# Splitting the weights into two float32r parts by transfers instead of by VectorE

## Chip, core and metric

The kernel runs on one core of a Trainium2 chip. The metric is the device time of one execution in microseconds; the median of two runs before the change is 1509.46 us (1509.07 and 1509.86). The profile is of one execution of its own, taken by the hardware profiler.

## What is computed

Two transformer blocks in a row on one sequence of 512 tokens and 1024 features, all in float32. The first has two mixers side by side (gated linear attention, and sparse attention with a compressed, a selected and a window branch), gates that merge them, and a SiLU feed-forward part 2816 wide. The second has two causal convolutions and stick-breaking attention as its mixer, and a squared-ReLU feed-forward part 4096 wide. Cut to the products with weights:

```python
proj = rms_norm(x, g) @ w_in                       # 1024 x 6440
x = x + rms_norm(mixed @ w_out, g_post)            # 1024 x 1024
f = (silu(h @ w_ffn_gate) * (h @ w_ffn_up)) @ w_ffn_down
p = _rmsnorm(x, g_attn) @ w_in_2
x = x + concat([y_a, y_b, y_c]) @ w_out_2
x = x + square(relu(h2 @ w_ff1_2)) @ w_ff2_2
```

## The kernel before

Every product is made as three float32r products: each operand is split into a high part (the value rounded to float32r) and a low part (what is left), and high by high, high by low and low by high are added up in PSUM. All weights are read from HBM once, in 228 pieces of 512 KB (a tile of 128 partitions x 1024 values), and three smaller pieces at the very start.

`load` (L122) makes one such piece. Its transfer (L125) is issued by SyncE into a staging tile `wst`, of which there are four. `split_w` (L110) then makes the high part `whi` by a casting copy on ScalarE (L113), and the low part `wlo` as `wst - whi` on VectorE (L114). There are four `whi` and four `wlo` as well, and they are given out in turn: the fifth piece takes the place of the first, once the products that read the first are done. Four weights of the second block go into tiles of their own, `early`, so that they can be split ahead of time.

Pieces have three shapes, by the stage that uses them. In the transposed projections (`proj_T`, L143, and `k_steps`, L157) a piece is 8 K tiles of 128 columns, 1024 rows of 512 bytes in HBM, and serves 24 matmuls of 512 columns. In the products in natural layout (`nat_half`, L215, and `half_steps`, L202) a piece is 2 K tiles of 512 columns, 256 rows of 2 KB; three or four pieces make a set, the set serves all four token tiles in turn, and so all pieces of a set are used until near the set's end. Eight pieces of the first block's output gate and four of `w_proj_nsa` are 4 K tiles of 256 columns, 512 rows of 1 KB. By shape there are 134, 82 and 12 pieces.

The kernel is written in program order, and a scheduler puts the instructions of each engine into that engine's queue; each queue is served in order. Beside the split, ScalarE and VectorE empty PSUM, make the activations and split those in the same way (`split_psum`, L135). GpSimd has the small steps of the norms (L240, L245, L246), masks and some set-up. The largest stages by weights are the first block's projections from the start on, its output projections and its feed-forward part (from about 395 to 905 us of the span), and the second block's feed-forward part (1105 to 1480 us); the attention stages lie between them.

Of the kernel before, what the change touches and what calls it, by code (L numbers as in the profile page):

```python
# [7 lines left out]
F32 = mybir.dt.float32  # L8
# [4 lines left out]
OP = mybir.AluOpType  # L13
# [7 lines left out]
def kernel(  # L21
# [78 lines left out]
    # the tensor engine's clock rises under load: products of zeros while the inputs are on their way  # L100
# [21 lines left out]
    def load(w, k0, kt, c0, n, step=1, pair=None):  # L122
        st = stage([128, kt, n])
        if step == 1:
            nc.sync.dma_start(st, w[k0 * 128:(k0 + kt) * 128, c0:c0 + n].rearrange("(k p) c -> p k c", p=128))  # L125
        else:
            for i in range(kt):
                k = k0 + i * step
                nc.sync.dma_start(st[:, i], w[k * 128:(k + 1) * 128, c0:c0 + n])
        return split_w(st, [128, kt, n], pair)  # L130
# [12 lines left out]
    def proj_T(acc, w, hT, cols=slice(0, 128), ts=slice(0, 512)):  # L143
        """acc[c, tok] = w[:, cols]^T h^T, the weights stationary."""
        wh, wl = w
        xh, xl = hT
        nk = wh.shape[1]
        for k in range(nk):
            mm(acc[:, ts], wh[:, k, cols], xh[:, k, ts], start=k == 0, stop=False)  # L149
            mm(acc[:, ts], wh[:, k, cols], xl[:, k, ts], start=False, stop=False)  # L150
            mm(acc[:, ts], wl[:, k, cols], xh[:, k, ts], start=False, stop=k == nk - 1)  # L151
# [5 lines left out]
    def k_steps(acc, w, hT):  # L157
        """the same, in steps of one K tile"""
        for k in range(8):
            mm(acc, w[0][:, k], hT[0][:, k], start=k == 0, stop=False)  # L160
            mm(acc, w[0][:, k], hT[1][:, k], start=False, stop=False)  # L161
            mm(acc, w[1][:, k], hT[0][:, k], start=False, stop=k == 7)  # L162
            yield

    def first_tiles(tiles, ahead=()):
        """The first products after a norm: all of the first 256 tokens, while the others are still on their way."""
        accs, ws = [], list(ahead)
        for i, (w, c0, tag) in enumerate(tiles):
            accs.append(ps(tag))
            if i >= len(ahead):  # L170
                ws.append(load_cols(w, c0))
            proj_T(accs[i], ws[i], hT, ts=slice(0, 256))
            if i in (0, 2):
                flush()
        for acc, w in zip(accs, ws):
            proj_T(acc, w, hT, ts=slice(256, 512))
        return accs

    def nat_mm(aT, acc, t, chunks, mid=lambda: None, cols=slice(None)):
        """acc[tok tile t, c] = sum_k a^T[k]^T w[k]; chunks: (list of k, split weights)"""  # L180
        s = slice(t * 128, (t + 1) * 128)
        seq = [(k, j, w) for ks, w in chunks for j, k in enumerate(ks)]
        for i, (k, j, (wh, wl)) in enumerate(seq):
            ah, al = aT(k)
            mm(acc, ah[:, s], wh[:, j, cols], start=i == 0, stop=False)  # L185
            mm(acc, ah[:, s], wl[:, j, cols], start=False, stop=False)  # L186
            mm(acc, al[:, s], wh[:, j, cols], start=False, stop=i == len(seq) - 1)  # L187
            if i == 1:
                mid()

    def nat_steps(aT, acc, t, chunks):
        """nat_mm in steps of one K tile"""
        s = slice(t * 128, (t + 1) * 128)
        seq = [(k, j, w) for ks, w in chunks for j, k in enumerate(ks)]
        for i, (k, j, (wh, wl)) in enumerate(seq):
            ah, al = aT(k)
            mm(acc, ah[:, s], wh[:, j, :], start=i == 0, stop=False)
            mm(acc, ah[:, s], wl[:, j, :], start=False, stop=False)
            mm(acc, al[:, s], wh[:, j, :], start=False, stop=i == len(seq) - 1)
            yield  # L200
# [9 lines left out]
    def natural(aT, w, ks, fin, c0=0, parts=None):  # L210
        """fin(t, half, acc) for both halves of 1024 columns, token tile by token tile."""
        for half in range(2):
            nat_half(aT, w, ks, fin, half, c0, parts)

    def nat_half(aT, w, ks, fin, half, c0=0, parts=None):  # L215
        chunks = []
        for i in range(0, len(ks), 2):
            kk = ks[i:i + 2]
            chunks.append((kk, load(w, kk[0], len(kk), c0 + half * 512, 512, step=max(kk[-1] - kk[0], 1))))
        for t in range(4):  # L220
            if t == 3 and half and parts:
                # in two, so that less is left to do after the last product
                for q in (slice(0, 256), slice(256, 512)):
                    acc = ps("mm", "nat")
                    nat_mm(aT, acc[:, q], t, chunks, cols=q)
                    parts(t, q, acc[:, q])
                return
            acc = ps("mm", "nat")
            nat_mm(aT, acc, t, chunks, lambda: flush(2))
            fin(t, half, acc)  # L230
# [4 lines left out]
    def half_sq(src, half, st):  # L235
        """mean of squares of one half row; eps goes in with the first half"""
        sq = small("sq")
        A.activation(ps("o", "junk"), src, AF.Square, scale=1.0 / 32, accum_out=sq)  # L238
        if half == 0:
            P.tensor_scalar(sq, sq, RMS_EPS, None, op0=OP.add)  # L240
        st[half] = sq
# [17 lines left out]
    def norm_T(t, g, hT):  # L259
        """RMS norm of token tile t of the residual, transposed into hT."""  # L260
# [18 lines left out]
    # transposes that wait for their norm: products that need not wait go first  # L279
# [9 lines left out]
    # =====================  block 1: mixers  =====================  # L289
# [86 lines left out]
    # transposed, with a row of ones for the bias  # L376
# [23 lines left out]
    def r_proj(hd):  # L400
        """x (1 + tanh(x / 2)) = 2 silu(x) of this head's output gate, natural layout"""
# [244 lines left out]
    def nsa_scores(h, bi):  # L646
        """softmax weights of one branch, gated; a step per query tile"""
# [27 lines left out]
    def nsa_values(h, bi):  # L675
        """the branch's weighted values, on top of the other branches'; a step per key tile and its products"""
# [46 lines left out]
    def merge_gates():  # L723
        """the gates of both mixers, in steps of one K tile"""
# [15 lines left out]
    # mn's tiles 2 p, 2 p + 1 take the place of the queries of heads 2 p, 2 p + 1  # L740
# [39 lines left out]
    for m in range(8):  # L780
# [3 lines left out]
        # the gated sum of both branches: one half of silu's and one of the gates' tanh form  # L784
# [7 lines left out]
    def post_norm_T(t, half, src, f, g, g_next, hT, st, eng):  # L792
        """x[t] += rms_norm(src) * g, then the next norm; src is one half of a token tile's row."""
# [22 lines left out]
    # =====================  block 1: FFN  =====================  # L816
    pc, tc3 = pool("pc")
    # 4 KB each: the first weights of block 2, then parts of its mixers' output
# [3 lines left out]
    # constants of block 2's mixers  # L822
# [66 lines left out]
    # =====================  block 2: mixers  =====================  # L889
    p3, t3 = pool("p3")  # L890
    # y^T as hi / lo: K tiles 0-1 the gated conv, 2-3 the GLU conv, 4-7 the attention
# [37 lines left out]
    def sb_scores(h):  # L929
        """stick-breaking weights of one head, a step per query tile"""  # L930
# [3 lines left out]
        for j in range(4):  # L934
# [10 lines left out]
            # log sigmoid(z); then -log a(s) = (z(s+1) - log a(s+1)) - log sigmoid(z(s)), from the masked end  # L945
# [8 lines left out]
    def sb_values(h):  # L954
        """the head's output: a step per key tile and its products, those one tile behind"""
# [54 lines left out]
    def log_sigmoid(dst, src, e):  # L1010
        """min(x, 0) - ln(1 + exp(-|x|))"""
        A.activation(e, src, AF.Abs)
        A.activation(e, e, AF.Exp, scale=-1.0)
        A.activation(e, e, AF.Ln, bias=1.0)
        V.scalar_tensor_tensor(dst, src, 0.0, e, OP.min, OP.subtract)
# [27 lines left out]
    def ln_steps():  # L1043
        ln = []
        for t in range(4):
# [8 lines left out]
            # the convolution's inputs are used up  # L1054
# [94 lines left out]
    # =====================  block 2: FFN  =====================  # L1149
# [87 lines left out]
```

## Time and profile before

| what | value |
|---|---|
| median of the two runs | 1509.46 us |
| the profiled execution: span from first to last instruction | 1504.9 us |
| own time of that execution, taken as span and the 4.6 us by which the median is longer | 1509.5 us |
| TensorE busy (matmuls) | 1487.9 us |
| VectorE busy | 765.6 us |
| ScalarE busy | 606.6 us |
| GpSimd busy | 62.9 us |
| moved by the DMA engines | 133.09 MB |

The profile's page has the busy times, the chain of work that ended last, groups of instructions by line, and the transfers with their time from issue to landing. The trace answers closer questions: the busy time of each engine in a stretch of the span, and the instructions of one engine in order of time with the idle time before each and what ended it. Matmuls overlap in their records, so their pace is read from their starts. Issuing a transfer isn't counted as busy time.

### The profile page before, as it was taken

The numbers are of one execution on the slowest core, as the hardware profiler recorded it, in microseconds if no ns is written. First come the engines' busy times: TensorE is split into PE (matmuls) and PEld (weight loads), VectorE is DVE, ScalarE is ACT, GpSimd is POOL, SyncE is SP. The second block draws the span as 40 slices with busy tenths as digits, with TensorE's granted clock in tenths as the row PEclk, the third lists the DMA queues.
The fourth block names the chain that finished last, engine by engine and source line by source line (L and its number), as shares of the span: only waits on it lengthen the run. The fifth ranks groups of instructions, "written<-read, shape, count | busy, mean of one in ns | idle before, by whom it ended". The sixth has DMA issues, their size and how long they took to land.

```text
span 1504.9 us, 18389 instructions
## 1 busy us (share of the span) xinstructions
PE 1487.9 (99%) x7220; PEld 1200.7 (80%) x7220; DVE 765.6 (51%) x1258; ACT 606.6 (40%) x1081; POOL 62.9 (4%) x177
## 2 busy tenths in 40 slices
PE   8999999999999999999999999999999999999998
PEld 6788888787788898878888888666689888888886
DVE  5244456867655463233333445979756344243343
ACT  6333224666632342322222334577734224142233
POOL 2000002000000010000000021000100000000000
PEclk9999999999999999999999999999999999999999
DMA  8242222221134243242243322211133242242321
GB/s 237 64 112 57 71 71 70 57 57 44 55 112 139 85 128 97 75 123 84 71 125 95 116 70 72 84 56 57 56 98 99 71 126 87 67 127 84 101 82 56
DMA packets 181278, 133.09 MB, mean 88 GB/s; under 512 B 11765, under 2 KB 157239, under 8 KB 181192
## 3 DMA queue, kind: packets, MB, share of 16 engines
q1 hardware_dynamic: 181192, 131.92, 30.2%
q8 instruction: 57, 0.93, 0.3%
q14 instruction: 29, 0.24, 0.1%
HBM read 129.80 MB, written 2.10 MB: 88 GB/s over the span
## 4 chain that ended last, share of the span: by engine, by line
PE 94%; DVE 2%; POOL 1%; ACT 1%; issue 1%; SPq 0%; DMA 0%; POOLq 0%; ACTq 0%; DVEq 0%
PE ps L149 13%; PE ps L151 13%; PE ps L150 13%; PE nat L187 9%; PE nat L186 9%; PE nat L185 9%; PE ps L162 4%; PE ps L161 4%; PE ps L160 4%; PE z L937 1%; PE pt L700 1%; PE ps L187 1%; PE ps L185 1%; PE ps L186 1%; PE o L693 1%; PE tp L273 1%
## 5 line engine op out<-in xcount | busy, mean ns | idle before, releaser
L113 ACT CAST whi<-wst 128x1024 fp32r<-128x1024 f32 (+1 forms) x229 | 239.1, 1046 | 493.6 <-PE ps L150 196.2
L114 DVE TENSOR_TENSOR wlo<-wst,whi 128x1024 fp32r<-128x1024 f32 (+1 forms) x229 | 279.5, 1222 | 287.1 <-ACT whi L113 283.4
L149 PE MATMUL ps<-hTh,whi 128*128 128x512 f32 (+1 forms) x880 | 331.4, 377 | 0.0
L150 PE MATMUL ps<-hTl,whi 128*128 128x512 f32 (+1 forms) x880 | 330.2, 375 | 0.0
L151 PE MATMUL ps<-hTh,wlo 128*128 128x512 f32 (+1 forms) x880 | 329.4, 374 | 0.0
L151 PEld LDWEIGHTS ps<-hTh,wlo 128*128 128x128 f32 x880 | 165.7, 188 | 31.9 <-DVE wlo L114 0.2
L149 PEld LDWEIGHTS ps<-hTh,whi 128*128 128x128 f32 x880 | 165.7, 188 | 31.6
L150 PEld LDWEIGHTS ps<-hTl,whi 128*128 128x128 f32 x880 | 165.8, 188 | 30.9
L187 PE MATMUL nat<-whi,al 128*128 128x512 f32 (+1 forms) x440 | 171.7, 390 | 0.0
L186 PE MATMUL nat<-wlo,ah 128*128 128x512 f32 (+1 forms) x440 | 171.4, 389 | 0.0
L185 PE MATMUL nat<-whi,ah 128*128 128x512 f32 (+1 forms) x440 | 170.9, 388 | 0.0
L160 PE MATMUL ps<-hTh,whi 128*128 128x512 f32 x240 | 98.0, 408 | 0.0
L186 PEld LDWEIGHTS nat<-wlo,ah 128*128 128x128 f32 x440 | 82.8, 188 | 18.6
L185 PEld LDWEIGHTS nat<-whi,ah 128*128 128x128 f32 x440 | 82.8, 188 | 18.3
L187 PEld LDWEIGHTS nat<-whi,al 128*128 128x128 f32 x440 | 82.8, 188 | 17.5
L161 PE MATMUL ps<-hTl,whi 128*128 128x512 f32 x240 | 96.2, 401 | 0.0
L162 PE MATMUL ps<-hTh,wlo 128*128 128x512 f32 x240 | 95.8, 399 | 0.0
L1087 DVE TENSOR_TENSOR xt<-xt,nat 128x512 f32<-128x512 f32 x43 | 29.5, 686 | 98.9 <-PE nat L187 97.6
L162 PEld LDWEIGHTS ps<-hTh,wlo 128*128 128x128 f32 x240 | 45.3, 189 | 8.8
L240 POOL TENSOR_SCALAR sq<-sq 128x1 f32<-128x1 f32 x28 | 9.4, 335 | 1015.9 <-ACT junk L238 1015.5
L865 DVE TENSOR_TENSOR sg<-sg,ps 128x512 f32<-128x512 f32 x22 | 15.2, 689 | 70.6 <-PE ps L151 69.9
L160 PEld LDWEIGHTS ps<-hTh,whi 128*128 128x128 f32 x240 | 45.4, 189 | 6.5
(351 smaller groups left out, 2194.8 us busy)
## 6 DMA issues: line engine op xcount, KB each, us to landing
wst<-in_w_in_dram SPq DMA_DIRECT2D x70, 512.0 KB, 3.9
wst<-in_w_ff_dram SPq DMA_DIRECT2D x64, 512.0 KB, 4.0
wst<-in_w_ffn_gate_dram SPq DMA_DIRECT2D x22, 512.0 KB, 4.0
wst<-in_w_ffn_up_dram SPq DMA_DIRECT2D x22, 512.0 KB, 4.0
wst<-in_w_ffn_down_dram SPq DMA_DIRECT2D x22, 512.0 KB, 3.8
wst<-in_w_out_dram SPq DMA_DIRECT2D x16, 512.0 KB, 3.9
xt<-in_x_dram SPq DMA_DIRECT2D x8, 512.0 KB, 3.6
wst<-in_w_proj_gla_dram SPq DMA_DIRECT2D x8, 512.0 KB, 3.6
```

The source lines that it names most:

```text
L113: A.copy(hi, st)
L114: lo_eng[0].tensor_tensor(out=lo, in0=st, in1=hi.bitcast(F32), op=OP.subtract)
L149: mm(acc[:, ts], wh[:, k, cols], xh[:, k, ts], start=k == 0, stop=False)
L150: mm(acc[:, ts], wh[:, k, cols], xl[:, k, ts], start=False, stop=False)
L151: mm(acc[:, ts], wl[:, k, cols], xh[:, k, ts], start=False, stop=k == nk - 1)
L160: mm(acc, w[0][:, k], hT[0][:, k], start=k == 0, stop=False)
L161: mm(acc, w[0][:, k], hT[1][:, k], start=False, stop=False)
L162: mm(acc, w[1][:, k], hT[0][:, k], start=False, stop=k == 7)
L185: mm(acc, ah[:, s], wh[:, j, cols], start=i == 0, stop=False)
L186: mm(acc, ah[:, s], wl[:, j, cols], start=False, stop=False)
L187: mm(acc, al[:, s], wh[:, j, cols], start=False, stop=i == len(seq) - 1)
L1087: V.tensor_tensor(X[t][:, HALF[half]], X[t][:, HALF[half]], acc, OP.add)
```

## The change

`load` no longer stages the weights and no longer calls `split_w`. GpSimd issues a first transfer straight from HBM into `whi`, whose type makes it a casting one; ScalarE writes the negative of `whi` into `wlo`; GpSimd issues a second transfer of the same weights from HBM, which is added to what stands in `wlo`. The three smaller pieces at the start are staged and split as before. All else in the diff is comments taken out, and lines after `load` have numbers that are larger by 5.

```diff
     def load(w, k0, kt, c0, n, step=1, pair=None):
-        st = stage([128, kt, n])
-        if step == 1:
-            nc.sync.dma_start(st, w[k0 * 128:(k0 + kt) * 128, c0:c0 + n].rearrange("(k p) c -> p k c", p=128))
-        else:
-            for i in range(kt):
-                k = k0 + i * step
-                nc.sync.dma_start(st[:, i], w[k * 128:(k + 1) * 128, c0:c0 + n])
-        return split_w(st, [128, kt, n], pair)
+
+        hi, lo = pair or (base.tile([128, kt, n], F32R, name="whi", tag="whi", bufs=4),
+                          base.tile([128, kt, n], F32R, name="wlo", tag="wlo", bufs=4))
+        ks = [k0 + i * step for i in range(kt)]
+        for i in range(1 if step == 1 else kt):
+            if step == 1:
+                src, h, l = w[k0 * 128:(k0 + kt) * 128, c0:c0 + n].rearrange("(k p) c -> p k c", p=128), hi, lo
+            else:
+                src, h, l = w[ks[i] * 128:(ks[i] + 1) * 128, c0:c0 + n], hi[:, i], lo[:, i]
+            P.dma_start(out=h, in_=src)
+            A.activation(l, h.bitcast(F32), AF.Copy, scale=-1.0)
+            P.dma_start(out=l, in_=src, accum_op=OP.add)
+        return hi, lo
```

The queues show where the pieces stand now. SyncE's queue before, in the second block's feed-forward part: the last two pieces of one `w_ff2` set, the four of the next, and the first of the following `w_ff1` pieces, one transfer each.

```order
L125 DMA wst_11052<-in_w_ff2_2_dram 128x2x512
L125 DMA wst_11058<-in_w_ff2_2_dram 128x2x512
L125 DMA wst_11168<-in_w_ff2_2_dram 128x2x512
L125 DMA wst_11174<-in_w_ff2_2_dram 128x2x512
L125 DMA wst_11180<-in_w_ff2_2_dram 128x2x512
L125 DMA wst_11186<-in_w_ff2_2_dram 128x2x512
L125 DMA wst_11297<-in_w_ff1_2_dram 128x8x128
```

GpSimd's queue of the changed kernel at the same place: L132 is the casting transfer and L134 the adding one.

```order
L132 DMA whi_10851<-in_w_ff2_2_dram 128x2x512
L134 DMA wlo_10852<-in_w_ff2_2_dram 128x2x512
L132 DMA whi_10960<-in_w_ff2_2_dram 128x2x512
L132 DMA whi_10965<-in_w_ff2_2_dram 128x2x512
L132 DMA whi_10970<-in_w_ff2_2_dram 128x2x512
L134 DMA wlo_10961<-in_w_ff2_2_dram 128x2x512
L134 DMA wlo_10966<-in_w_ff2_2_dram 128x2x512
L134 DMA wlo_10971<-in_w_ff2_2_dram 128x2x512
L132 DMA whi_10975<-in_w_ff2_2_dram 128x2x512
L134 DMA wlo_10976<-in_w_ff2_2_dram 128x2x512
L132 DMA whi_11085<-in_w_ff1_2_dram 128x8x128
```

Each piece now stands in one queue twice, and the second transfer of the set's first piece stands behind the first transfers of its second and third. In the whole program GpSimd has 456 such transfers, 228 of each kind, and goes 147 times from a run of L132 to a run of L134.

ScalarE's queue of the changed kernel shortly ahead of that place: L133 is the negation, L1171 and L1174 are the relu and the high part of an activation.

```order
L133 ACTIVATE wlo_10842<-whi_10841 128x1024
L1171 ACTIVATE rl_10792<-ps_10762 128x512
L1174 CAST ah_10795<-rl_10792 128x512
L133 ACTIVATE wlo_10847<-whi_10846 128x1024
L1171 ACTIVATE rl_10829<-ps_10799 128x512
L1174 CAST ah_10832<-rl_10829 128x512
L133 ACTIVATE wlo_10852<-whi_10851 128x1024
```

The negations stand where the casts (L113) stood, between the steps that empty PSUM; before, the VectorE subtraction followed them on another queue.

## Rows read from the trace of the kernel before

**Rows 1.** The page: busy time, share of the span, instructions.
```profile
PE 1487.9 (99%) x7220; PEld 1200.7 (80%) x7220; DVE 765.6 (51%) x1258; ACT 606.6 (40%) x1081; POOL 62.9 (4%) x177
```
**Rows 2.** The page: chain that ended last, share of the span by engine.
```profile
PE 94%; DVE 2%; POOL 1%; ACT 1%; issue 1%; SPq 0%; DMA 0%; POOLq 0%; ACTq 0%; DVEq 0%
```
**Rows 3.** Groups by shape, VectorE and ScalarE: count, busy us, mean ns, idle before.
```profile
L114 DVE TENSOR_TENSOR wlo<-wst,whi 128x1024 fp32r<-128x1024 f32 x226 | 276.6, 1226 | 287.1 <-ACT whi L113 283.4
...
L113 ACT CAST whi<-wst 128x1024 fp32r<-128x1024 f32 x226 | 236.6, 1048 | 492.6 <-PE ps L150 196.2 <-PE nat L187 150.3 <-issue 104.3
```
**Rows 4.** Busy time by stretch; PE, PEld, DVE, ACT, POOL, PEclk, DMA share, GB/s.
```profile
780.30:802.60 22.30, 22.30 (x97) 18.09 (x96) 7.47 (x8) 6.34 (x8) 0.00 (x0) 1.00 0.33 95
```
**Rows 5.** Page: transfers by source, count, KB each, median us to landing; and the queue.
```profile
q1 hardware_dynamic: 181192, 131.92, 30.2%
...
wst<-in_w_ff_dram SPq DMA_DIRECT2D x64, 512.0 KB, 4.0
wst<-in_w_ffn_gate_dram SPq DMA_DIRECT2D x22, 512.0 KB, 4.0
```
**Rows 6.** SyncE's transfers of L125: duration of the issue in ns, min/median/max.
```profile
L125 SPq DMA_DIRECT2D wst<-in_w_ffn_gate_dram x22: 367/368/402, 509.6 to 813.8; - x22
L125 SPq DMA_DIRECT2D wst<-in_w_ffn_down_dram x22: 367/368/368, 568.2 to 864.0; - x22
```
**Rows 7.** Groups by shape, GpSimd.
```profile
L240 POOL TENSOR_SCALAR sq<-sq 128x1 f32<-128x1 f32 x28 | 9.4, 335 | 1015.9 <-ACT junk L238 1015.5
...
L795 POOL TENSOR_TENSOR FA<-FA,gain 128x512 f32<-128x512 f32 x4 | 5.2, 1294 | 0.3
L605 POOL TENSOR_SCALAR biasc<-negc 128x128 f32<-128x128 f32 x8 | 4.8, 616 | 0.3
```
**Rows 8.** ScalarE at the end of a `w_ff2` half: start us, duration, instruction, idle before.
```profile
1204.12 1.05 ACT L113 CAST whi<-wst 128x1024 fp32r<-128x1024 f32 x1 [14.80 <-PE nat L187]
1205.56 1.05 ACT L113 CAST whi<-wst 128x1024 fp32r<-128x1024 f32 x1 [0.39 <-PE nat L187]
1206.94 1.05 ACT L113 CAST whi<-wst 128x1024 fp32r<-128x1024 f32 x1 [0.33 <-PE nat L187]
1208.33 1.05 ACT L113 CAST whi<-wst 128x1024 fp32r<-128x1024 f32 x1 [0.34 <-PE nat L187]
```
**Rows 9.** What TensorE waited for: us in total, times, longest.
```profile
PE tp L273 <- DVE xn L267: 4.3, 6, 1.4
PE ps L185 <- ACT hTh L137: 1.7, 1, 1.7
...
PE ps L186 <- DVE wlo L114: 0.8, 1, 0.8
```
**Rows 10.** Busy time by stretch near the start; columns as in rows 4.
```profile
10.00:15.00 5.00, 2.87 (x14) 2.44 (x15) 4.47 (x6) 3.80 (x7) 0.50 (x1) 0.87 0.93 254
15.00:20.00 5.00, 4.82 (x29) 4.56 (x27) 2.61 (x6) 3.19 (x9) 1.31 (x4) 0.78 0.97 329
```
**Rows 11.** Busy time of the three densest stages, by stretch; columns as in rows 4.
```profile
1105.00:1480.00 375.00, 375.00 (x1729) 309.17 (x1728) 160.51 (x189) 118.07 (x164) 5.96 (x16) 1.00 0.31 92
500.00:905.00 405.00, 403.21 (x1857) 331.37 (x1857) 155.13 (x175) 126.55 (x189) 20.82 (x43) 1.00 0.33 97
395.00:500.00 105.00, 105.00 (x482) 84.60 (x481) 57.71 (x93) 37.69 (x60) 0.23 (x1) 1.00 0.36 111
```

## The prediction

> **What bounds the kernel now.** I read the busy times first, then the chain that ended last, then what TensorE waited for, and last the stretches where weights are densest. TensorE is busy for 1487.9 of 1504.9 us [rows 1], its instructions are 94% of the chain [rows 2], and the one wait for a low part of a weight on its list is 0.8 us [rows 9]. So the reader is to see a kernel with 17 us of room (1504.9 - 1487.9, 1.1%): whatever is taken off VectorE, no more than that can come back. The two steps of the split, 226 of 1048 ns and 226 of 1226 ns [rows 3], lie beside matmuls.
>
> The pace to be kept stands in one stretch of the feed-forward part [rows 4]: 97 matmuls started in 22.30 us, 0.23 us each, so a piece of 24 matmuls lasts 5.57 us; four pieces were loaded in that stretch at a DMA share of 0.33, so one transfer of 512 KB costs all 16 engines 0.33 x 22.30 / 4 = 1.84 us. It lands 4.0 us after its issue [rows 5]. Today that latency shows nowhere, because the four staging tiles are filled ahead: when a high part's place comes free, only 1.05 + 1.23 us are left to do [rows 3, 8].
>
> **The change part by part.**
>
> *Removed:* 276.6 us of VectorE [rows 3], all beside matmuls, and the 0.8 us wait: -2 us at most with what hangs on it. ScalarE's step stays (a negation of the same 128x1024; I take the 1.05 us of the cast). SyncE's issues go.
>
> *The lead.* The staging tiles are out of the path, so nothing can be fetched before the place of the piece four back is free. From there it is now one transfer, one negation, a second transfer. The second transfer has to read the weight and what it adds to; counting both reads, I take its engine time as 2 x 1.84 = 3.7 us. No row shows one; the lower bound is 1.84 us, the rate of a plain transfer, and as an upper bound I take four times, 7.4 us.
>
> *GpSimd's issue.* No row shows a transfer issued there. The nearest from below is SyncE's 0.37 us, whatever the number of rows [rows 6]. GpSimd's own work runs at 1294 / 512 = 2.5 ns per column in one group and 616 / 128 = 4.8 ns in another [rows 7]. If it writes up the rows of a transfer one after the other, 1024 rows cost up to 0.37 + 1024 x 4.8 ns = 5.3 us. I take 2.5 ns, the larger and longer operation: 2.9 us for 1024 rows, 1.7 for 512, 1.0 for 256.
>
> The Trainium skill speaks to both prices. "DMA: Bandwidth & Descriptors", section "Anatomy of one DMA — SWDGE (gpsimd) path", calls the generation small and gives 2.0 us + bytes at 436 GB/s for a whole transfer, which for 512 KB would be 3.2 us, an estimate; no run here shows it. "Collectives: The Full Stack", section "The bandwidth ceiling: the fold count and why AG ≠ RS ≠ AR", holds that an adding transfer is slower because of its two reads and not because of the addition, with half the rate; by it the second transfer would cost the 3.7 us. By the first page alone the next term falls away and the sum would be the first rival's.
>
> *Term 1, the queue of GpSimd.* It is served in order, and a low part's transfer waits until the high part has landed and been negated: 4.0 + 1.05 = 5.05 us in each of the 147 changes from a run of L132 to a run of L134, 147 x 5.05 / 228 = 3.3 us per piece. For a piece of 1024 rows that and two issues are 3.3 + 2 x 2.9 = 9.1 us against the 5.57 us in which TensorE uses it up: 3.55 us too slow. What stands behind the waiting transfer are the next piece's high part and the norms' small steps, and on ScalarE the steps that empty PSUM stand behind the negation, so TensorE waits for all of them. Of the 134 such pieces 84 are in the three dense stages (8 of `w_proj_gla`, 44 of gate and up, 32 of `w_ff1`), where TensorE is busy all the time [rows 11]: 84 x 3.55 = 298 us. The other 50 are among the 76 pieces of the remaining 620 us (1505 - 885), 8.2 us per piece; I put them at nothing, and they cost when the issue is dearer. Pieces of 256 rows fit: 3.3 + 2.0 = 5.3 us.
>
> *Term 2, turnovers.* A set in natural layout holds its places to its last token tile: the four come free 1.4 us apart, the first 18 matmuls or 4.2 us ahead of the end [rows 8]. Before, 2.3 us were needed from there. Now three first transfers are issued first (the third waits for a place free only 1.4 us before the end), and the fourth piece comes after three second transfers. With the 3.7 us, six transfers keep the engines until 12 us past the end (3 x 1.84 + 3 x 3.7 - 4.2); the fourth piece's first transfer lands at about 16, its low part at about 23, and the next set wants it at 4.2: a stall of 19 us. With 1.84 us and 0.37 us an issue the same count gives 12. I take 15 us for the 11 sets that follow a set; 6 us for the 10 that are followed by other pieces, each of which lasts 5.57 us; 8 us for the 10 that follow such pieces, where only the fourth is late. Together 11 x 15 + 10 x 6 + 10 x 8 = 305 us. Low: 218 us (12, 3 and 5.6).
>
> *Term 3, the clock.* Near the start TensorE was idle for 2.1 of 5 us, and the granted clock fell to 0.87 and then 0.78 in a stretch where it was busy again [rows 10], a mean over the levels of 2.4 and 1.2 GHz. 0.22 x 5 us is 1.1 us lost; with twice that at 20 of the long stalls, 40 us. Nothing below zero; it could be several times that if TensorE stays half busy.
>
> **Sum.** The profiled execution's 1509.5 us (its span and 4.6 us; the median of the runs is 1509.46): 1509.5 - 2 + 298 + 305 + 40 = 2150 us.
>
> **Rivals.**
>
> *The issue is cheap.* At 0.37 us an issue the queue needs 3.3 + 0.7 = 4.0 us per piece, less than 5.57, and term 1 is gone. For it: 1024 rows cost SyncE no more than 256 [rows 6]. Against: there the transfers come from another engine. What is left is term 2, 218 to 305 us, and half the clock's: 1747 to 1835 us; 1780. If the engines take the second transfer as a plain one and the stalls come out at half, 1640.
>
> *The transfers or the issue are dearer.* At four times, a piece takes 1.84 + 7.4 = 9.2 us of all engines: the 152 pieces of the dense stages 1398 us instead of the 885 [rows 11], and the other 76 pieces 699 in the remaining 620: 1509 + 513 + 79 + 305 = 2410. At 5.3 us an issue, 3.3 + 10.6 = 13.8 us per piece of 1024 rows: 84 x 8.2 = 690 us, and the other 76 pieces 50 x 13.8 + 26 x 7.5 = 885 in 620, another 265: 1509 + 690 + 265 + 305 + 40 = 2810. For it: no row speaks against an adding transfer being far slower. I put it at 2600.
>
> *Not slower: all is hidden.* Four places are a lead of three pieces, 16.7 us, and one piece's chain is 4.0 + 1.05 + 4.0 + two issues of 0.37 = 9.8 us; if the queue lets the chains overlap, steady stages lose nothing, and the turnovers are the only place. It decides where the low part of the next set lands within the 4.2 us, or the scheduler's order of products gives TensorE other work there. Price: between the 17 us of room and a few waits, 1495 to 1535 us; 1510. Against it: 9.8 is over twice 4.2, and nothing can be fetched sooner [rows 8].
>
> **How the numbers follow.** The forecast (1950 to 2400 us) has 0.45, cheap issues 0.24, dearer ones 0.26, not slower 0.05. The range, 1640 to 2950 us, leaves out the last and the outer ends of the two others, together 0.2 or less. About 2% is what a measurement of this kernel can tell from no change: faster by more 0.01 (the room is 1.1%), within it 0.04, slower 0.95.
>
> **What would show it.** Right: L114 is left with three instructions; TensorE's waits are led by transfers into `wlo` and `whi`, and its share falls to about 70%; GpSimd's queue has no idle stretch in the dense stages other than waits for ScalarE; a `w_ff1` piece lasts about 9 us instead of 5.57, and the first product of each new set waits for over 10. Wrong in size: transfers from GpSimd whose issue lasts about 0.4 us (first rival), or engines busy at 90% and more throughout with landings far over 6 us (second). Wrong altogether: TensorE still at 97% or more.

## The result, and the profile after

The changed kernel takes 1999.2 us (median of 1993.58 and 2004.83) where the kernel before took 1509.46: a ratio of 1.3245, interval 1.3156 to 1.3334. So it is slower, by 490 us; forecast were 2150 in a range from 1640 to 2950.

First the page, in the order of [rows 1, 2, 5]: busy time, the chain that ended last, the queue of GpSimd's transfers, and what they took to land.

```profile
PE 1650.1 (82%) x7220; PEld 1282.9 (64%) x7220; DVE 503.6 (25%) x1030; ACT 601.2 (30%) x1081; POOL 573.2 (29%) x633
...
issue 16%; DMA 9%; PE 8%; POOL 4%; ACT 2%; DVE 1%; POOLq 0%; ACTq 0%
...
q0 software_dynamic: 336000, 239.10, 73.4%
...
whi<-in_w_ff_dram POOLq DMA_DIRECT2D x64, 512.0 KB, 6.7
wlo<-in_w_ff_dram POOLq DMA_DIRECT2D x64, 512.0 KB, 6.6
```

TensorE's 94% of the chain [rows 2] are down to 8%. Its idle time went from 17 to 353 us (2003.1 - 1650.1), and its own busy time rose by 162 us for the same 7220 matmuls (1650.1 - 1487.9): 336 + 162 make the 498 us between the two spans. A landing takes 6.7 us instead of 4.0 [rows 5], and each piece now needs two, one behind the other.

What the engines waited for (us in total, times, longest), TensorE first, then GpSimd; for TensorE this stands against [rows 9]:

```profile
PE nat L191 <- DMA wlo<-in_w_ff_dram: 80.5, 24, 8.2
PE nat L191 <- DMA wlo<-in_w_ffn_down_dram: 47.2, 14, 6.6
PE ps L156 <- DMA wlo<-in_w_ffn_gate_dram: 25.7, 9, 6.5
...
PE ps L154 <- DMA whi<-in_w_ff_dram: 12.4, 10, 2.7
```
```profile
POOL wlo L134 <- ACT wlo L133: 720.8, 162, 11.0
POOL whi L132 <- PE nat L192: 197.7, 43, 17.2
POOL whi L132 <- PE ps L156: 87.6, 23, 14.9
```

All lines of TensorE's list add up to 345 us in 160 waits: 248 us in 83 are for low parts (158 in 48 in natural layout, nearly all of the other 90 in transposed products), 30 in 28 for high parts, 67 in 49 for ScalarE or VectorE. Before, the one wait for a low part was 0.8 us, and those for ScalarE or VectorE were 10 us in 14. GpSimd stands 720.8 us at 162 of its adding transfers, waiting for the negation; with those that the trace puts down to other steps of ScalarE it is 849 us at 191.

The chain inside a piece can be read in the second block's feed-forward part. GpSimd's rows (start, us, instruction, idle before) and then ScalarE's; DMA_DIRECT2D is the issuing of a transfer, which on GpSimd, other than on SyncE, is counted as busy time:

```profile
1768.62 1.58 POOL L134 DMA_DIRECT2D wlo<-in_w_ff_dram  x1 [1.18 <-ACT wlo L133]
1769.51 1.60 POOL L132 DMA_DIRECT2D whi<-in_w_ff_dram  x1
1778.56 1.54 POOL L134 DMA_DIRECT2D wlo<-in_w_ff_dram  x1 [7.45 <-ACT wlo L133]
1779.46 2.10 POOL L132 DMA_DIRECT2D whi<-in_w_ff_dram  x2
```
```profile
1748.85 1.06 ACT L133 ACTIVATE wlo<-whi 128x1024 fp32r<-128x1024 f32 x1 [10.29 <-DMA whi<-in_w_ff_dram]
...
1753.39 1.06 ACT L133 ACTIVATE wlo<-whi 128x1024 fp32r<-128x1024 f32 x1 [1.62 <-DMA whi<-in_w_ff_dram]
...
1764.43 1.06 ACT L133 ACTIVATE wlo<-whi 128x1024 fp32r<-128x1024 f32 x1 [8.12 <-DMA whi<-in_w_ff_dram]
...
1767.26 1.06 ACT L133 ACTIVATE wlo<-whi 128x1024 fp32r<-128x1024 f32 x1
...
1777.11 1.06 ACT L133 ACTIVATE wlo<-whi 128x1024 fp32r<-128x1024 f32 x1 [6.93 <-DMA whi<-in_w_ff_dram]
1778.08 0.58 ACT L1171 ACTIVATE rl<-ps 128x512 f32<-128x512 f32 x1
```

The casting transfer issued at 1769.51 ends ScalarE's wait at 1777.11, 7.6 us later. Only then does the adding transfer go (1778.56), and the next casting ones stood behind it (1779.46). On ScalarE the step that empties PSUM, L1171, follows the negation without idle time: it stood behind it. From 1748.85 to 1777.11, all in `w_ff1`, there are four steps from one negation to the next, 7.1 us each on average ((1777.11 - 1748.85) / 4), where the products want a piece every 5.57 us [rows 4]. Over the last three groups of eight `w_ff1` pieces, from the first L1171 to the last, it is 7.2 to 7.3 us.

The stalls then cost a second time. Busy time by stretch, around one stall before a low part (PE with its matmuls, granted clock, DMA share, GB/s), and single matmuls in it:

```profile
1690.00:1695.00 5.00, 4.20 (x17) 1.00 0.73 204
1695.00:1700.00 5.00, 0.00 (x0) 0.82 0.91 195
1700.00:1705.00 5.00, 1.94 (x5) 0.50 1.10 186
1705.00:1710.00 5.00, 5.00 (x16) 0.65 0.57 150
1710.00:1715.00 5.00, 5.00 (x23) 1.00 0.41 54
```
```profile
1703.06 0.80 PE L191 MATMUL nat<-wlo,ah 128*128 128x512 f32 x1 [8.22 <-DMA wlo<-in_w_ff_dram]
1703.66 0.63 PE L192 MATMUL nat<-whi,al 128*128 128x512 f32 x1
...
1708.35 0.46 PE L192 MATMUL nat<-whi,al 128*128 128x512 f32 x1
...
1709.11 0.39 PE L191 MATMUL nat<-wlo,ah 128*128 128x512 f32 x1
1709.34 0.40 PE L192 MATMUL nat<-whi,al 128*128 128x512 f32 x1
```

After 8.22 idle us the granted clock is 0.50, the level of 1.2 GHz; the next twelve matmuls start 0.44 us apart instead of 0.23 ((1708.35 - 1703.06) / 12), and then 2.4 GHz is back. The columns 1.00, 0.82, 0.50, 0.65, 1.00 are this one stall.

### The profile page after: what moved, and what is told of

Its sections match the earlier page's. It is cut to its first block, busy times and chain, and to the rows that moved or that the text cites. A ratio compares the mean times of both kernels' runs of the same rounds, so it can differ in the third digit from the quotient of the medians.

```text
span 2003.1 us, 18519 instructions
## 1 busy us (share of the span) xinstructions
PE 1650.1 (82%) x7220; PEld 1282.9 (64%) x7220; DVE 503.6 (25%) x1030; ACT 601.2 (30%) x1081; POOL 573.2 (29%) x633
## 5 line engine op out<-in xcount | busy, mean ns | idle before, releaser
L133 ACT ACTIVATE wlo<-whi 128x1024 fp32r<-128x1024 f32 x226 | 239.2, 1058 | 1007.0 <-DMA whi<-in_w_ff_dram 351.3
L156 PE MATMUL ps<-hTh,wlo 128*128 128x512 f32 (+1 forms) x880 | 351.6, 401 | 82.1 <-DMA wlo<-in_w_ffn_gate_dram 25.7
L154 PE MATMUL ps<-hTh,whi 128*128 128x512 f32 (+1 forms) x880 | 351.5, 399 | 31.1 <-DMA whi<-in_w_ff_dram 12.4
L191 PE MATMUL nat<-wlo,ah 128*128 128x512 f32 (+1 forms) x440 | 196.1, 446 | 127.8 <-DMA wlo<-in_w_ff_dram 80.5
L156 PEld LDWEIGHTS ps<-hTh,wlo 128*128 128x128 f32 x880 | 178.0, 203 | 129.6 <-DMA wlo<-in_w_ffn_gate_dram 29.5
L154 PEld LDWEIGHTS ps<-hTh,whi 128*128 128x128 f32 x880 | 179.2, 204 | 71.4 <-issue 21.9
L134 POOL DMA_DIRECT2D wlo<-in_w_in_dram x68 | 99.8, 1475 | 240.8 <-ACT wlo L133 160.9
L134 POOL DMA_DIRECT2D wlo<-in_w_ff_dram x64 | 88.8, 1394 | 221.0 <-ACT wlo L133 220.7
L132 POOL DMA_DIRECT2D whi<-in_w_in_dram x68 | 69.5, 1032 | 145.5 <-PE ps L167 41.8
L132 POOL DMA_DIRECT2D whi<-in_w_ff_dram x64 | 67.8, 1090 | 145.9 <-PE nat L192 98.8
L1092 DVE TENSOR_TENSOR xt<-xt,nat 128x512 f32<-128x512 f32 x43 | 29.6, 688 | 247.4 <-PE nat L192 240.8
```

The source lines that it names most:

```text
L132: P.dma_start(out=h, in_=src)
L133: A.activation(l, h.bitcast(F32), AF.Copy, scale=-1.0)
L134: P.dma_start(out=l, in_=src, accum_op=OP.add)
```

## Experiments

Twelve kernels. The question of the first four is whether the time is lost to the transfers' rate (theory B) or to the chain, the queue and the lead (theory A).

**Transfers alone.** Weight pieces of 512 KB one after the other, nothing else.

```python
for i in range(16):
    P.dma_start(out=v8(T[i]), in_=rows1024(i))                       # L100, casting
...
for i in range(16):
    P.dma_start(out=v8(T[i]), in_=rows1024(i), accum_op=OP.add)      # L104, adding
```

> This kernel leaves out the whole computation and makes only transfers, sixteen of 512 KB in each of eight stretches, each stretch begun when the last has landed: plain from SyncE, then from GpSimd plain, casting, adding into float32r and adding into float32 (rows of 512 bytes), then plain, casting and adding (rows of 2 KB). Theory A (the 490 us come from the chain of two transfers and a negation behind a place that comes free late, and from GpSimd's one queue): the engines take 1.8 us for a plain transfer, about 2 for a casting one and 3.7 to 4.6 for an adding one, in all the 6.4 us per piece that the changed kernel's 73.4% share gives; the issue on GpSimd is 0.7 to 1.6 us. Theory B (the DMA engines are the bound because adding is slow): an adding transfer takes 5 us or more of all engines, in every stretch of adding, with GpSimd idle.

VectorE reads each tile as it lands (start, us, instruction, idle before); the first two rows are of casting, the next two of adding transfers, all of 1024 rows:

```profile
86.11 0.16 DVE L88 TENSOR_TENSOR flag<-flag,t 128x1 f32<-128x1 f32 x1 [1.65 <-DMA t<-in_w_ff_dram]
87.91 0.16 DVE L88 TENSOR_TENSOR flag<-flag,t 128x1 f32<-128x1 f32 x1 [1.65 <-DMA t<-in_w_ff_dram]
...
123.92 0.16 DVE L88 TENSOR_TENSOR flag<-flag,t 128x1 f32<-128x1 f32 x1 [2.71 <-DMA t<-in_w_ff_dram]
126.80 0.16 DVE L88 TENSOR_TENSOR flag<-flag,t 128x1 f32<-128x1 f32 x1 [2.73 <-DMA t<-in_w_ff_dram]
```

Casting: 1.81 us a transfer, the same as plain ones from GpSimd or SyncE, and near the 1.84 us of before [rows 4]. Adding: 2.89 us, 1.6 times as much; with 256 rows of 2 KB it is 2.5 against 1.36. An issue took GpSimd 0.88 us for 1024 rows and 0.70 for 256, 1.54 and 1.18 with the addition. One piece is 1.81 + 2.89 = 4.7 us, below the 5.57: by rate alone the dense stages could have kept their pace. The adding transfer is far below the 5 us of theory B, and below the 3.7 to 4.6 of theory A too.

The Trainium skill, "Collectives: The Full Stack", section "The bandwidth ceiling: the fold count and why AG ≠ RS ≠ AR", puts ReduceScatter in a ring at half of AllGather's rate because its addition needs two reads. Here, on one core, an adding transfer takes 1.6 and 1.85 times as long as a casting one, so that ratio is an upper end.

**Without the addition.** The second transfer overwrites; the low part is then the weight itself.

```diff
-            P.dma_start(out=l, in_=src, accum_op=OP.add)
+            P.dma_start(out=l, in_=src)
```

> The second transfer overwrites the negation instead of being added to it, so the low part of every weight is the whole weight rounded and the output isn't that of the reference; the waits, the queue and the order are those of the changed kernel. Theory A: the chain is the same but for the adding, so the time falls by less than half of the 490 us, to 1800 to 1950 us. Theory B: with the slow addition gone the engines are far from full, and the time falls below 1700 us.

1774.52 us, ratio 1.1766 (1.1718 to 1.1813): 225 us less. Landings into `wlo` fall to 4.4 to 4.9 us in the large groups (6.0 to 6.6 in the changed kernel), and GpSimd's transfers stand in the same order. It came between the two theories.

**The casting transfer alone.** `whi` by the new transfer, `wlo` as before from a staged copy.

```diff
...
+            nc.sync.dma_start(s, src)
             P.dma_start(out=h, in_=src)
...
+        V.tensor_tensor(lo, st, hi.bitcast(F32), OP.subtract)
```

> The casting transfer alone: the high part comes by GpSimd's casting transfer, the low part by VectorE's subtraction from a copy that SyncE stages ahead, as before. Theory A: nothing on GpSimd's queue waits for another engine's step any more, and what follows a place that comes free is one transfer of about 5 us and 1.2 us: steady stages at the old pace, turnovers of 2 to 4 us each: 1550 to 1650 us. Theory B: 3.6 us of the engines per piece and no adding: below 1560 us. If the casting itself is what is slow: above 1750 us.

1618.41 us, ratio 1.0731 (1.0693 to 1.0769). As theory A expected. This is the fastest version with a part of the change that still makes the whole result; none here beats the kernel before.

**The adding transfer alone.** Staged copy, cast and negation on ScalarE, then the adding transfer.

```diff
...
+            nc.sync.dma_start(s, src)
...
+        A.copy(hi, st)
+        A.activation(lo, hi.bitcast(F32), AF.Copy, scale=-1.0)
+        for src, l in srcs:
             P.dma_start(out=l, in_=src, accum_op=OP.add)
```

> The adding transfer alone: SyncE stages the weights ahead and ScalarE makes the high part by its cast as before, then the negation, and GpSimd's adding transfer makes the low part. Theory A: from a free place on it is 1.05 + 1.05 + 6.3 us; steady stages lose little, turnovers 4 to 8 us each: 1600 to 1720 us. Theory B: the engines take about as long as in the changed kernel per piece (1.8 + the adding), so the time stays above 1800 us.

1753.45 us, ratio 1.1626 (1.1561 to 1.1691), a little above what A expected: a transfer that waits for a step on staged data is by itself worth half of the loss (1753 - 1509 = 244 us), though the staged copy is fetched ahead again. ScalarE has both steps here, 815 us busy instead of 601; what that adds wasn't separated.

**The next cast ahead of this addition.** In the dense stages the program issues the casting transfer of the next piece before the adding transfer of this one.

```diff
...
+    def in_turn(jobs):
+        p = load_hi(*jobs[0])
+        for nxt in jobs[1:] + [None]:
+            q = load_hi(*nxt) if nxt else None
+            yield load_lo(*p)
+            p = q
...
```

> The changed kernel, but in the dense stages (first tiles, gate and up, w_ff1, and every natural layout product) the casting transfer of the next piece is issued before the adding transfer of this one; places, ScalarE and the bytes stay. Theory Q (GpSimd's queue runs in order: it stood 721 us at 162 adding transfers waiting for ScalarE's negation, and the next casting transfer stood behind them): a w_ff1 piece falls from some 10 us toward the 6.45 us that the transfers took of the engines, 1700 to 1870 us, and the wait for ScalarE before an adding transfer shrinks to under 400 us in all. Theory P (four places give too little lead, so that the next casting transfer could not begin earlier anyway): 1930 to 2010. Theory B (the DMA engines are full): 1940 to 2010.

2003.75 us, ratio 1.3279 (1.3255 to 1.3304): no change. The queue says why this decides little: in the trace GpSimd's order differs from the changed kernel's in 108 of 456 positions, by small shifts, and goes from L132 to the adding line 147 times as before; the scheduler had already put casting transfers ahead. It hardly tested the queue.

**Six places.** `whi` and `wlo` with six places instead of four; the staging tiles give their memory.

```diff
...
-        hi, lo = pair or (base.tile([128, kt, n], F32R, name="whi", tag="whi", bufs=4),
-                          base.tile([128, kt, n], F32R, name="wlo", tag="wlo", bufs=4))
+        hi, lo = pair or (base.tile([128, kt, n], F32R, name="whi", tag="whi", bufs=6),
+                          base.tile([128, kt, n], F32R, name="wlo", tag="wlo", bufs=6))
...
```

> The changed kernel with six places of each part instead of four (the staging tiles, which it hardly uses, give their memory). Theory P (lead): GpSimd's waits for PE to free a place, 285 us in all, mostly go, and PE's stalls with them: 1700 to 1850. Theory Q (the chain in GpSimd's queue sets the pace of a piece): the waits for a place turn into waits for ScalarE, and only the sets' first pieces gain: 1880 to 1980. Theory B (engines full): 1940 to 2010.

1864.89 us, ratio 1.2357 (1.2321 to 1.2393): 134 us less, which neither theory B nor Q allows, and just short of the best for P. Its waits (GpSimd, then TensorE):

```profile
POOL wlo L134 <- ACT wlo L133: 777.3, 166, 11.7
...
POOL whi L132 <- PE ps L156: 28.6, 10, 11.7
```
```profile
PE ps L154 <- ACT sg L869: 31.5, 8, 9.3
PE nat L191 <- DMA wlo<-in_w_ffn_down_dram: 25.8, 5, 7.3
PE nat L191 <- DMA wlo<-in_w_ff_dram: 24.0, 13, 4.2
```

GpSimd's wait for ScalarE stays. TensorE's waits for low parts go from 248 to 76 us, but those for ScalarE or VectorE rise from 67 to 188: with more lead the weights are there, and what is late is ScalarE, whose queue stands at a negation while PSUM waits to be emptied. Its rows, and TensorE's next one, show it (L869 is the activation of the first feed-forward part):

```profile
1051.82 1.06 ACT L133 ACTIVATE wlo<-whi 128x1024 fp32r<-128x1024 f32 x1 [8.18 <-DMA whi<-in_w_ffn_up_dram]
1052.78 0.58 ACT L869 ACTIVATE sg<-ps 128x512 f32<-128x512 f32 x1
...
1053.41 0.80 PE L154 MATMUL ps<-hTh,whi 128*128 128x512 f32 x1 [8.16 <-ACT sg L869]
```

The negation waited 8.18 us for a landing, L869 came right behind it, and TensorE stood 8.16 us until L869 was done. So a landing can stop TensorE by way of ScalarE's queue, without any weight that TensorE itself waits for.

**The negation on VectorE.**

```diff
-            A.activation(l, h.bitcast(F32), AF.Copy, scale=-1.0)
+            V.tensor_scalar(l, h.bitcast(F32), -1.0, None, op0=OP.mult)
```

> The changed kernel with the negation on VectorE instead of ScalarE, everything else kept. Theory S (the negation stands in ScalarE's in-order queue behind work that waits for PE, so PE's stalls and the pieces' feed each other): below 1900, and GpSimd's wait before an adding transfer below 500 us in all. Theories Q, P and B: the negation waits for the landing of the casting transfer on whichever engine; within 2.5% of the changed kernel, 1950 to 2050.

2066.43 us, ratio 1.3693 (1.3665 to 1.372): slower still, by 67 us, which no theory expected; S falls. The negation itself is shorter (717 ns against 1058), and the landings are the same. VectorE's rows show its queue standing at the negation in the same way:

```profile
1748.63 0.69 DVE L133 TENSOR_SCALAR wlo<-whi 128x1024 fp32r<-128x1024 f32 x1 [5.34 <-DMA whi<-in_w_ff_dram]
1749.24 0.68 DVE L1092 TENSOR_TENSOR xt<-xt,nat 128x512 f32<-128x512 f32 x1
```

L1092, which empties PSUM, came without idle time behind it. Whether that makes the 67 us was not tried; it stays open.

**Both, six places and the turned order.** The edits of "Six places" and of "The next cast ahead of this addition" together.

> Both: six places, and the next piece's casting transfer ahead of this one's adding transfer. Theories Q and P together (what is lost is lead and order, not rate): 1560 to 1750, TensorE's granted clock at 0.95 or above. Theory B (the rate of the transfers, 6.45 us of the engines a piece): not below 1850.

1879.62 us, ratio 1.2451 (1.2396 to 1.2506): that of six places, within a per cent. The turned order again does nothing. Theories Q and P together, with 1560 to 1750, fail; theory B, with not below 1850, isn't denied by this run, only by those above.

Theories Q, P and B had thus each been denied something, and the wait for the landing of the first transfer had not been taken away in any run. Two of the last four kernels do that, and a third does in its free pairs.

**Pieces in isolation.** The computation left out; pairs of transfers that depend on nothing, then chains in places of their own, then chains in four places that are free at once; the first two also beside 200 products.

```python
P.dma_start(out=h, in_=rows(i))
if neg:
    A.activation(l, h.bitcast(F32), AF.Copy, scale=-1.0)
P.dma_start(out=l, in_=rows(i), accum_op=OP.add)
```

> The computation is left out: only weight pieces of 1024 rows (a casting transfer and an adding one, 512 KB each). Six stretches, three of them twice: 12 pieces whose two transfers depend on nothing and stand in turn in the queue; 12 pieces with the negation between the two transfers, each piece in a place of its own; 24 pieces with the negation in four places, freed as soon as a piece has landed; in the second half the first two with 200 products on TensorE beside them. Theory R (the transfers' own rate bounds): every stretch takes what the transfers take alone, 1.81 + 2.89 = 4.7 us a piece, the four places at most 5.5. Theory L (the chain of landing, negation and landing bounds once places are few): the free pairs 4.7, the four places 7 to 10. Theory E (TensorE's reads of SBUF slow the transfers): the stretches with products over 5.5 a piece, those without 4.7.

VectorE's rows, one for each piece that has landed: two of the free pairs, then two of the four places, twelve pieces apart; and the stretches (PE, PEld, DVE, ACT, POOL, clock, DMA share, GB/s) of free pairs, four places, and free pairs beside products:

```profile
42.13 0.16 DVE L86 TENSOR_TENSOR flag<-flag,h 128x1 f32<-128x1 f32 x1 [4.17 <-DMA h<-in_w_ff_dram]
46.47 0.16 DVE L86 TENSOR_TENSOR flag<-flag,h 128x1 f32<-128x1 f32 x1 [4.17 <-DMA h<-in_w_ff_dram]
...
180.21 0.16 DVE L120 TENSOR_TENSOR ya<-h,l 128x1 fp32r<-128x1 f32 x1 [9.70 <-DMA l<-in_w_ff_dram]
...
247.24 0.16 DVE L120 TENSOR_TENSOR ya<-h,l 128x1 fp32r<-128x1 f32 x1 [9.95 <-DMA l<-in_w_ff_dram]
```
```profile
30.00:66.00 36.00, 0.00 (x0) 0.00 (x0) 2.60 (x17) 0.00 (x0) 12.35 (x11) 1.00 1.54 229
160.00:280.00 120.00, 0.00 (x0) 0.00 (x0) 5.88 (x38) 21.12 (x20) 49.60 (x41) 1.00 1.46 185
316.00:345.00 29.00, 29.00 (x130) 24.02 (x129) 0.47 (x3) 0.00 (x0) 11.15 (x9) 1.00 1.58 236
```

Free pairs take 4.33 us a piece, with TensorE busy or not (229 and 236 GB/s): the products don't slow the transfers, and theory E falls. With the chain in four places it is (247.24 - 180.21) / 12 = 5.59 us, although every place is free the moment its piece has landed. That is already all of the 5.57 us; in the kernel the place is also held while the products read it. The third theory, L (the chain inside a piece, in too few places), expected 7 to 10 us here and R at most 5.5, so this stretch alone didn't settle it. With a place for each piece, GpSimd still stood 27.7 us in three waits for the negation (3.83, 13.96 and 9.90), so its queue waits without any lack of places; that stretch, 70.1 us for twelve pieces with its start, is too short to give a pace.

**No wait for the landing.** ScalarE writes zeros into `wlo` from a constant, so that the adding transfer needn't wait; the low part is the weight itself.

```diff
-            A.activation(l, h.bitcast(F32), AF.Copy, scale=-1.0)
+            A.activation(l, nhalf[:, 0:1].to_broadcast([128, *l.shape[1:]]), AF.Copy, scale=0.0)
```

> The changed kernel with the negation's input replaced by a resident constant times zero: ScalarE still writes the low tile and the transfer adds the weight to it, but nothing waits for the casting transfer to land; the low part is the weight itself, so the result is left out. Bytes, transfers, places and ScalarE's work stay. Theory L (the chain of landing and negation inside each piece): 1700 to 1870 us. Theory R (the transfers' rate) with theory P (few places): 1940 to 2010, with the waits for ScalarE turned into waits for a place.

1691.54 us, ratio 1.1199 (1.1163 to 1.1235): 308 us less with the same transfers, bytes, places and ScalarE steps: a little below the range of L, and far from R. GpSimd's waits change places:

```profile
POOL whi L132 <- PE ps L156: 287.6, 95, 15.3
POOL whi L132 <- PE nat L192: 254.0, 16, 23.4
POOL whi L132 <- PE ps L167: 129.3, 24, 8.4
POOL wlo L134 <- ACT wlo L133: 104.7, 111, 5.1
```

It now waits for places, 671 us in the first three lines, and that is a queue ahead of its consumer: TensorE's share is 92%. The scheduler also orders GpSimd's queue anew when this dependence is gone: in the trace it goes from a casting to an adding transfer 227 times instead of 147. What this does belongs to the 308.

**No wait, six places**, and **six places, no addition**: the edits above, combined.

> The same with six places (low part the weight itself, result left out). Theory L: clearly under the 1865 of six places with the chain, 1560 to 1740. Theory R: 1820 to 1880, the queue's landings no shorter.

1564.61 us, ratio 1.0373 (1.0358 to 1.0389), TensorE at 97%, its granted clock 0.985: at the lower edge of what L expected, far from R. TensorE's waits for ScalarE or VectorE fall to 12 us from the 188 of six places, those for low parts to 29 from 76.

> Six places, and the second transfer overwrites the negation and adds nothing (low part the weight itself, result left out). Four places without the adding took 1775. Theory R (rate): with 2 x 1.81 = 3.6 us a piece below the 5.57 us that the products take, and lead, most is gone: 1560 to 1680. Theory L: the chain stays, 1700 to 1780.

1658.06 us, ratio 1.1000 (1.0957 to 1.1043), within what R expected and below L's range.

Medians side by side, in us:

| | four places | six places | difference |
|---|---|---|---|
| the changed kernel | 1999.2 | 1864.9 | 134 |
| second transfer without the addition | 1774.5 | 1658.1 | 116 |
| no wait for the first landing | 1691.5 | 1564.6 | 127 |

The parts nearly add up: the wait inside a piece costs 308 us (300 with six places), the addition 225 (207) as long as that wait is there, two places are worth 116 to 134. Chain and addition aren't two sums: without the wait, all adding transfers stay and only 182 us (1691.5 - 1509.5) are left; with six places 55. So with six places at most 55 of the addition's 207 us can be there without the wait, if the time doesn't fall below that of the kernel before: it costs mostly by making the chain longer (landings into `wlo` of 6.0 to 6.6 us instead of 4.4 to 4.9, by four places), not by filling the engines. With four places that bound is 182 of 225, which says little.

The cause that these runs show is latency against lead: two landings in a row, about 6.7 us each, begun only when a place comes free. Without the wait between them and with two more places, 435 of the 490 us are gone. Not separated is what the wait does in three ways at once: it lengthens a piece, it holds up what stands behind in GpSimd's queue, and it holds up the steps behind the negation on ScalarE. Nor is it shown how the 182 us split between few places and the two transfers' rate, beyond the 127 us that two more places give back.

## Why the prediction was right, and where its sizes were off

- *Sign, place and mechanism*: right. TensorE's waits are led by transfers into `wlo`, TensorE's share fell to 82% (70% forecast), VectorE's saved time (765.6 to 503.6 us) bought nothing, and the lost lead and the in-order chain carry the loss, as the runs without the wait and with six places show. Forecast were +641 us in three terms, and +490 came.
- *The wait in GpSimd's queue*: near. 147 changes of 5.05 us made 742; the trace has 162 waits for the negation with 720.8 us, and 849 us in 191 with all that it puts down to ScalarE. Taking the wait away gives back 308 us, where term 1 said 298. Part of that agreement is luck, by the next point.
- *The issue at 2.9 us* failed: 0.9 us for a casting and 1.55 for an adding transfer of 1024 rows (0.70 and 1.18 us for 256). GpSimd was busy for 29% of the span. By the term's own sum a piece of 1024 rows would then need 3.3 + 2.45 = 5.75 us, 0.2 above the pace; that it still lasted 7.1 goes with a wait for places, which the term didn't have, and with landings longer than the 4.0 us that it took. The groups (busy, mean ns, idle before) of the `w_ff` pieces:

```profile
L134 POOL DMA_DIRECT2D wlo<-in_w_ff_dram x64 | 88.8, 1394 | 221.0 <-ACT wlo L133 220.7
...
L132 POOL DMA_DIRECT2D whi<-in_w_ff_dram x64 | 67.8, 1090 | 145.9 <-PE nat L192 98.8
```

  A piece costs GpSimd (88.8 + 221.0 + 67.8 + 145.9) / 64 = 8.2 us: 2.45 of issues, 3.45 of waiting for ScalarE and 2.3 mostly for a place. Half of these pieces have 1024 rows and half 256, for which 9.1 and 5.3 were forecast, 7.2 on average: 3.9 of issues and 3.3 of waiting. The tell-tale "no idle stretch other than waits for ScalarE" was wrong, and a `w_ff1` piece lasted 7.1 us instead of 9.
- *Landings at 4.0 us* failed the other way: 5.4 to 7.9 us into `whi` in the large groups. These two errors pulled against each other.
- *Term 1 as a stall*: 298 us forecast. TensorE waited some 90 us for low parts in transposed products, 30 for high parts, and 67 for ScalarE or VectorE (10 before), 187 together. The overrun per piece was mis-sized: 7.1 - 5.57 = 1.5 us in the group shown, instead of 3.55.
- *Term 2, turnovers*: oversized, 305 against 158 us in natural layout. The single longest wait was 8.2 us; none over 10. The addition was taken as 3.7 us and is 2.5 for pieces of this shape.
- *Term 3, the clock*: undersized fourfold, 40 against 162 us more busy time. Its price per stall was about right (1.1 to 2.2 us forecast; the stall shown above loses 2.5, twelve steps of 0.44 instead of 0.23). Its count of 20 was wrong: there were 83 waits for low parts, and 162 / 83 is 2.0 us each. That the term "could be several times that" was its own warning.
- *The rivals*. "The issue is cheap" named the true size of an issue better than the forecast, but its 1780 lies 219 us below the result, farther off than the forecast's 151 above: its ground, that the queue then keeps up, fell, since the wait in it was worth 308 us with issues at 0.9 to 1.55. "The transfers or the issue are dearer" is excluded by 2.89 us for an adding transfer and 1.55 for its issue. "Not slower" fell as expected: with the landings of the `w_ff` pieces the chain is 6.7 + 1.06 + 6.6 us and 2.45 of issues, 16.8 us, as long as the whole lead of 16.7 us that it counted on.
- The Trainium skill, "DMA: Bandwidth & Descriptors", section "Anatomy of one DMA — SWDGE (gpsimd) path", calls the generation small and gave the estimate of 3.2 us for a transfer. On the first it was nearer than my 2.9 us; its 3.2 us has no row here: in the changed kernel the groups' median landings run from 4.1 us (four casting transfers of `w_proj_nsa`) to 8.8.

## What to carry to other kernels

A step saved on an engine that is not the bottleneck buys nothing, and replacing it by a second transfer that depends on the first puts two landings behind the moment a place comes free. Before such a change, compare the lead (places times the use of a piece) with the whole chain to readiness, landings taken from a loaded run, and count stalls twice: once as idle time and once as the slower clock behind each. Staging tiles that look redundant can be the lead itself. And look at what stands behind the waiting step in its engine's queue: here it was the emptying of PSUM.

## What the hardware showed beyond expectation

- Casting in the transfer costs nothing in rate: 1.81 us for 512 KB, as a plain one. Adding costs 1.6 times that at 512-byte rows and 1.85 times at 2 KB rows; float32 and float32r tiles, tried at 512-byte rows, are alike.
- Casting and adding transfers in turn took 4.33 us a pair, less than the 4.7 us of the two alone.
- The DMA share is no measure of full engines: it read 1.54 in the free pairs, where transfers lay over each other, and 0.8 to 1.08 in dense stretches of the changed kernel at 139 to 153 GB/s, while 229 GB/s were to be had.
